# Hybrid RG-LRU / HGRN2 decoder layer on one core: the mixer's instructions noted down and issued in a list-scheduled order, elementwise work moved between engines

## The chip, the core and the metric

One Trainium2 chip, one of its cores. The metric is the device time of one execution in microseconds (us). A core has TensorE (PE: matmuls; PEld is its weight load), VectorE (DVE), ScalarE (ACT), GpSimd (POOL) and SyncE (SP, which here only issues DMAs). Each of them carries out its own instructions strictly in the order of its queue.

## The reference

One decoder layer over x (1024 tokens x 1024 channels, float32):

```python
h = rms_norm(x, norm_mix)
proj = h @ w_in                                  # 1024 -> 8 groups of 1024
xa, ga, q, f, v, g, m_a, m_b = split(proj)
xa = causal_depthwise_conv(xa)                   # width 4
r, i = sigmoid(xa @ w_r + b_r), sigmoid(xa @ w_i + b_i)      # four blocks of 256
log_a = -8 * r * softplus(-lam)
h_t = exp(log_a) * h_(t-1) + sqrt(-expm1(2 * log_a)) * (i * xa)   # RG-LRU
y_a = h * gelu(ga)
f_gate = lb + (1 - lb) * sigmoid(f); k = (1 - lb) * sigmoid(-f)
o = rms_norm(linear attention of silu(q), k, decay f_gate, v)      # HGRN2, 8 heads of 128
y_b = o * silu(g)
x = x + (sigmoid(m_a) * y_a + sigmoid(m_b) * y_b) @ w_out
x = x + square(relu(rms_norm(x) @ w_up)) @ w_down
out = rms_norm(x)
```

## The kernel before

Every float32 matmul is done as three (`mm3`): both operands are split into a high part (ACT, L87) and a rest (DVE, L88). Large products go by a seven-product scheme over 2x2 blocks (`PLAN`): a **quad** is 256 output columns of a weight matrix, cut into four blocks, and takes 7 steps of 12 matmuls of 128x512, 84 in all.

The program has these stages: norm of x and the projection of v; the **mixer**, 28 quads of w_in (`MIX`: XA gives xa for two heads, QF gives q and f of one head, GM gives g and m_b, GA gives m_a and ga); the output projection (`out_proj`, matmuls `po<-wH,y`) with the second norm; MLP up; MLP down with the final norm. `quad_steps` loads the weights of a mixer quad: two tiles are sums of two blocks, made by a load from SP's queue and an accumulating DMA from POOL's queue (`s<-quads_in`, L240 and L241), the rest of the sums is on DVE (L252, L253), then come the splits.

Beside the quads run twelve **tasks** and eight **merges**. `gated_recurrence(p)` (four times) takes two heads of xa: convolution (L441 and L450), gate matmuls (`pr`, `pi`), then sigmoid, exp, tanh, sqrt on ACT with arithmetic between on DVE (L484 to L488), and the scan over time (L498), once for each half of the sequence. `hgrn(u)` (eight times) takes one head of q and f: it folds decays into q and k on DVE (all under `mul`, L506), makes score blocks with small matmuls (`sc`), transposes k (`pk`), makes states (`pkv`, then `ks` on DVE), reads them (`po<-v,scT` and `po<-ks,qf`), norms (squares L692, mean L696, power -1/2 on POOL L697, scaling L699) and transposes back (`poT`), first for the first half of the sequence and then for the second. A task's results go to DRAM (`od`, `hd`), the gates as well (`mad`, `mbd`); `merge(u)` loads them back, multiplies and adds on DVE (L717, L720), splits (L721, L722) and stores `yd`, which `load_y` fetches for the output projection. The tasks use one tile pool `m` with one buffer for each tile name, so a task can begin with a tile only when the task before has let go of it.

The order before is that of the framework's scheduler: it takes the calls in source order, with quad work at a raised priority (`K_EV`, `K_PREP`), and by its own estimate of times.

Of the kernel before, what the change touches and what calls it, by code (L numbers as in the profile page):

```python
# [18 lines left out]
P = 128  # L19
# [35 lines left out]

@with_exitstack
def trunk(ctx: ExitStack, tc: tile.TileContext, x, wts, quads, pv, gains, mask_f, mask_u, out):
    nc = tc.nc
    V, A, G, PE = nc.vector, nc.scalar, nc.gpsimd, nc.tensor

    const = ctx.enter_context(tc.tile_pool(name="const", bufs=1))
    wp = ctx.enter_context(tc.tile_pool(name="wp", bufs=1))
    ps = ctx.enter_context(tc.tile_pool(name="ps", bufs=1, space=PSUM))
    dram = ctx.enter_context(tc.tile_pool(name="dram", bufs=1, space=DRAM))

    def opened(name, **how):
        cm = tc.tile_pool(name=name, bufs=1, reuse_waits="tile", **how)
        return cm.__enter__(), lambda: cm.__exit__(None, None, None)
# [21 lines left out]
    def raw_tile(name):  # L90
        return wp.tile([P, 1024], F32, tag="raw", name=name, bufs=3)

    def load_w(i):
        raw = raw_tile(f"raw{i}")
        nc.sync.dma_start(raw, wts[i])
        return raw
# [124 lines left out]
    def quad_steps(i, pools, raws=raw_tile, singles=2, adding=False):  # L221
# [8 lines left out]
        def load(k):  # L230
            if adding and k == 0:
                raw[k] = pools[0].tile([P, 512], F32, tag="a11", name=f"q{i}{k}")
                nc.sync.dma_start(raw[k], quads[i, k][:, 0:512])
            else:
                raw[k] = raws(f"q{i}{k}")
                nc.sync.dma_start(raw[k], quads[i, k])

        def added(k):
            s[k] = raws(f"s{i}{k}")
            nc.sync.dma_start(s[k][:, 0:512], halves(quads[i, 0])[1])  # L240
            G.dma_start(s[k][:, 0:512], halves(quads[i, 1 - k])[1 - k], accum_op=ALU.add)  # L241
# [46 lines left out]
    hopp, close_hop = opened("hop", side="right")  # L288
    hop = {o: [hopp.tile([P, 4, T], F32R, tag=o + q, name=f"h{o}{q}") for q in ("H", "L")] for _, _, o in PLAN}
# [12 lines left out]
    def load_x(r):  # L302
        x_in[r] = st.tile([P, D], F32, tag="x", name=f"x{r}", bufs=2)
        nc.sync.dma_start(x_in[r], x[r * P : (r + 1) * P, :])
# [34 lines left out]
    nc.sync.dma_start(pvt, pv)  # L339
    nc.sync.dma_start(mf, mask_f)  # L340
    mu32 = st.tile([P, 7, 32], F32, tag="mu32", name="mu32")
    nc.sync.dma_start(mu32, mask_u)
# [15 lines left out]
    def project_v(c, hf, beside):  # L358
# [24 lines left out]
        for tt in range(4):  # L383
            vt = st.tile([P, 512], F32, tag="vt", name=f"vt{c}{hf}{tt}", bufs=2)
            A.copy(vt, pp[tt])
            nc.sync.dma_start(v_d[hf][:, :, 4 * c + tt, :], vt.rearrange("p (h d) -> p h d", h=4))
# [28 lines left out]
    ev, close_ev = opened("ev", side="right")  # L415
    hcar = const.tile([P, 8], F32, tag="hcar", name="hcar")
# [5 lines left out]
    def gated_recurrence(p):  # L422

        xp = [mt(t, f"xp{2 * p + s}", (P, 1792)) for s, t in enumerate(("q1", "qa"))]
        for s in range(2):
            G.memset(xp[s][:, 0:3], 0.0)
            nc.sync.dma_start(xp[s][:, 3 : S + 3], xa_d[2 * p + s])
        wi = mt("v", f"wi{p}", (P, 2, T))
        raw = wi.rearrange("p s t -> p (s t)")
        nc.sync.dma_start(raw, wts[V_TILES + p])  # L430
        wh, wl = (mt(t, f"rg{p}{t}", (P, 1024), F32R) for t in ("ks", "scT"))
        split(raw, wh, wl)
        seg = mt("seg", f"xc{p}", (P, 1536))
        xc = seg[:, 0:1024].rearrange("p (s t) -> p s t", s=2)
        xh = mt("f", f"xcH{p}", (P, 2, T), F32R)
        xl = mt("kk", f"xcL{p}", (P, 2, T), F32R)
        for c in range(NC):
            at = c * T
            for s in range(2):
                u = 2 * p + s  # L440
                V.tensor_scalar(  # L441
                    xc[:, s, :],
# [6 lines left out]
                for j in range(3):  # L449
                    V.scalar_tensor_tensor(  # L450
                        xc[:, s, :],
                        xp[s][:, at + j : at + j + T],
                        pvt[:, PV_CW + 8 * j + u : PV_CW + 8 * j + u + 1],
                        xc[:, s, :],
# [3 lines left out]
            split(xc, xh, xl)  # L458

            parts = [  # L460
                (wi[:, 0, :], wi[:, 1, :], seg[:, 1024:1536], xc[:, 0, :]),
                (*(t[:, 1032 : 1032 + T] for t in xp), m.tile([P, T], F32, tag="o", name=f"e{c}{p}"), xc[:, 1, :]),
            ]
            for s in range(2):
                u = 2 * p + s
                w, ig, e, t = parts[s]
                pr, pi = bank("sc", f"pr{c}{u}"), bank("sc", f"pi{c}{u}")
                for o, k0 in ((pr, 0), (pi, 2)):
                    for k in range(2):
                        cols = slice((k0 + k) * 256 + s * P, (k0 + k) * 256 + (s + 1) * P)  # L470
                        mm3(o, wh[:, cols], wl[:, cols], xh[:, k, :], xl[:, k, :], k == 0, k == 1)
                A.activation(w, pr, AF.Sigmoid, bias=pvt[:, PV_BR + u : PV_BR + u + 1])
                A.activation(ig, pi, AF.Sigmoid, bias=pvt[:, PV_BI + u : PV_BI + u + 1])
                V.tensor_tensor(out=ig, in0=ig, in1=t, op=ALU.mult)


            for s in range(2):
                u = 2 * p + s
                w, ig, e, t = parts[s]
                A.activation(e, w, AF.Exp, scale=sp4n[:, u : u + 1])  # L480
                A.activation(w, w, AF.Tanh, scale=sp4[:, u : u + 1])
            for s in range(2):
                w, ig, e, t = parts[s]
                V.tensor_scalar(w, w, 0.0, None, op0=ALU.max)  # L484
                V.tensor_scalar(e, e, 1.0, None, op0=ALU.add)
# [3 lines left out]
            for s in range(2):  # L489
                w, ig, e, t = parts[s]  # L490
                A.activation(w, w, AF.Sqrt)
            for s in range(2):
                u = 2 * p + s
                w, ig, e, t = parts[s]
# [6 lines left out]
                nc.sync.dma_start(h_d[u][:, at : at + T], h)  # L501

    def hgrn(u):
# [3 lines left out]
        qr = mt("qa", f"qr{nm}", (P, 1792))[:, 0:S]  # L507
        nc.sync.dma_start(qr, q_d[u])
        f = mt("f", f"f{nm}", (P, S))
        kk = mt("kk", f"kk{nm}", (P, S))  # L510
        nc.sync.dma_start(f, f_d[u])
        v = mt("v", f"v{nm}", (P, 8, P))
        nc.sync.dma_start(v, v_d[u // 4][:, u % 4])
        scT = mt("scT", f"scT{nm}", (P, 8, P))
        G.memset(scT, 0.0)
# [5 lines left out]
        V.tensor_scalar(f, f, omlb[:, u : u + 1], lb[:, u : u + 1], op0=ALU.mult, op1=ALU.add)  # L521
        V.tensor_scalar(kk, kk, omlb[:, u : u + 1], None, op0=ALU.mult)
# [83 lines left out]
        qv = qb[:, :, 0:32]  # L606
        for b in range(4):
# [52 lines left out]
        state = lambda n: ks[:, 4 + n % 4, :]  # L660
# [3 lines left out]
        for half in range(2):  # L664
            n0, nkv = 4 * half, 4 - half
            pks.append(bank("hg", f"pk{half}{u}"))
            for n in range(nkv):
                PE.transpose(pks[half][:, n * P : (n + 1) * P], kk[:, (n0 + n) * P : (n0 + n + 1) * P], ident)
        for half in range(2):
            n0, nkv = 4 * half, 4 - half  # L670
            on = mt("on", f"on{half}{u}", (P, 4, P))
            A.copy(ks[:, :nkv, :], pks[half][:, : nkv * P].rearrange("p (n k) -> p n k", n=nkv))
            pkv = bank("sc", f"pkv{half}{u}")
            for n in range(nkv):
                PE.matmul(pkv[:, n * P : (n + 1) * P], ks[:, n, :], v[:, n0 + n, :], start=True, stop=True)
            po = bank("hg", f"po{half}{u}")
            for n in range(4):
                a = n0 + n
                o_ps = po[:, n * P : (n + 1) * P]
                PE.matmul(o_ps, scT[:, a, :], v[:, a, :], start=True, stop=a == 0)  # L680
                if a > 0:
                    PE.matmul(o_ps, qf[:, a * P : (a + 1) * P], state(a), start=False, stop=True)  # L682
                if n < nkv:
                    kv = pkv[:, n * P : (n + 1) * P]
                    if a == 0:
                        V.tensor_copy(state(1), kv)
                    else:
                        V.scalar_tensor_tensor(
# [520 lines left out]
```

## Time and profile before

| what | value |
|---|---|
| three runs | 1695.49, 1706.29, 1712.78 us; median 1706.29 |
| the profiled execution | 1699.1 us, its span 1697.3 us |
| busy in the span | PE 1563.2, DVE 1242.3, ACT 839.5, POOL 128.1 us |
| mean granted TensorE clock | 0.973 |

In the profile a row of a group gives line, engine, operation, output and inputs, shape, count, then busy time in us and mean ns of one, then the idle time of that engine just before them and who ended it. A row of a timeline gives start, duration and the instruction. A stretch `a:b` is in us from the start of the span; in the table of stretches the busy times of the engines follow in the order PE, PEld, DVE, ACT, POOL, then the granted clock, the DMA share and GB/s.

### The profile page before, as it was taken

Reading aid. Unit: us, or ns where it says so; the run is one execution under the profiler, and the core shown is the slowest. Engines: PE = TensorE matmul, PEld = TensorE weight load, DVE = VectorE, ACT = ScalarE, POOL = GpSimd, SP = SyncE. Lnnn points to the kernel's source line nnn. Section 1 sums busy time; section 2 is a strip of 40 time slices with the busy share of each in tenths; the row PEclk is TensorE's granted clock in tenths of the full one; section 3 lists DMA queues with packets and bytes.
Section 4 is the critical chain, followed back from the end, with each engine's and each line's share of the span. In section 5 each row is a group of like instructions: output and inputs, shape, how many; then the busy total and the mean of one; then the engine's idle time right before and its main releaser. Section 6 shows DMA issues by size and latency. Waiting matters only on the chain.

```text
span 1697.3 us, 22898 instructions
## 1 busy us (share of the span) xinstructions
PE 1563.2 (92%) x8520; PEld 1242.5 (73%) x8520; DVE 1242.3 (73%) x1908; ACT 839.5 (49%) x1335; POOL 128.1 (8%) x169
## 2 busy tenths in 40 slices
PE   6999899988899799998999687999999999999998
PEld 4787677766677577776777566788778778888886
DVE  4755687778777786898455259788777798787877
ACT  5644545754476455744433146666766652212213
POOL 0000122111211111112100001000000000000000
PEclk9999999999999999999999798999999999999999
DMA  5554463465444646455357684366566666566652
GB/s 184 163 151 152 130 183 111 121 181 170 147 136 154 175 142 193 125 158 162 116 167 273 224 300 163 124 257 251 226 239 253 237 233 262 223 239 261 248 231 100
DMA packets 110799, 320.96 MB, mean 189 GB/s; under 512 B 11872, under 2 KB 20192, under 8 KB 99936
## 3 DMA queue, kind: packets, MB, share of 16 engines
q1 hardware_dynamic: 101040, 299.05, 49.1%
q0 software_dynamic: 8064, 14.68, 5.4%
q10 hardware_dynamic: 1584, 5.77, 0.9%
q8 instruction: 67, 1.10, 0.3%
q14 instruction: 44, 0.36, 0.1%
HBM read 217.75 MB, written 101.71 MB: 188 GB/s over the span
## 4 chain that ended last, share of the span: by engine, by line
PE 43%; DMA 11%; DVE 9%; ACT 4%; issue 3%; POOL 1%; SPq 0%; DVEq 0%; POOLq 0%; ACTq 0%
PE dX L126 3%; PE dX L128 3%; PE dX L127 3%; PE uX L126 3%; PE uX L127 3%; PE uX L128 3%; DMA q<-quads_in 3%; DMA s<-quads_in 2%; PE dY L128 2%; PE dY L126 2%; PE dY L127 2%; PE uY L128 2%; PE uY L126 2%; PE uY L127 2%; DMA raw<-wts_in 1%
## 5 line engine op out<-in xcount | busy, mean ns | idle before, releaser
L1124 DVE TENSOR_TENSOR acc<-acc,dX 128x512 f32<-128x512 f32 x128 | 85.2, 684 | 31.1 <-PE dX L128 30.4
L87 ACT CAST wA<-q 128x512 fp32r<-128x512 f32 x60 | 37.1, 621 | 137.0 <-PE dX L128 102.4
L241 POOL DMA_DIRECT2D s<-quads_in x56 | 51.5, 920 | 441.0 <-DMA s<-quads_in 124.9
L252 DVE TENSOR_TENSOR s<-s,q 128x512 f32<-128x512 f32 x60 | 41.4, 689 | 56.4 <-DMA s<-quads_in 51.7
L87 ACT CAST wH<-raw 128x1024 fp32r<-128x1024 f32 x40 | 42.0, 1051 | 66.1 <-PE po L127 30.1
L88 DVE TENSOR_TENSOR wL<-raw,wH 128x1024 fp32r<-128x1024 f32 x40 | 48.9, 1223 | 34.8 <-ACT wH L87 34.4
L126 PE MATMUL po<-wH,y 128*128 128x512 f32 x128 | 53.2, 421 | 18.7 <-DMA y<-yd 8.6
L253 DVE TENSOR_TENSOR s<-s,q 128x512 f32<-128x512 f32 x60 | 41.3, 688 | 29.7 <-DMA q<-quads_in 29.5
L88 DVE TENSOR_TENSOR wA<-q,wA 128x512 fp32r<-128x512 f32 x60 | 41.2, 686 | 20.5 <-ACT wA L87 20.5
L1124 DVE TENSOR_TENSOR acc<-acc,dY 128x512 f32<-128x512 f32 x64 | 43.5, 686 | 16.3 <-PE dY L128 15.3
L127 PE MATMUL po<-wL,y 128*128 128x512 f32 x128 | 53.3, 416 | 0.3 <-DVE wL L88 0.3
L128 PE MATMUL po<-wH,y 128*128 128x512 f32 x128 | 52.2, 408 | 0.0
L983 ACT ACTIVATE b<-b 128x512 f32<-128x512 f32 x48 | 30.3, 632 | 36.1 <-DVE b L982 36.1
L126 PEld LDWEIGHTS po<-wH,y 128*128 128x128 f32 x128 | 25.5, 200 | 26.0 <-DMA y<-yd 9.0
L450 DVE SCALAR_TENSOR_TENSOR xc<-xp,pvt,xc 128x512 f32<-128x512 f32 x48 | 35.4, 745 | 0.5
L692 ACT ACTIVATE on<-po 128x128 f32<-128x128 f32 x64 | 16.9, 280 | 28.8 <-PE po L682 28.7
L984 ACT ACTIVATE b<-b 128x512 f32<-128x512 f32 x48 | 30.2, 631 | 1.3
L127 PEld LDWEIGHTS po<-wL,y 128*128 128x128 f32 x128 | 26.0, 203 | 6.5 <-DVE wL L88 1.3
L702 PE MATMUL poT<-ident,on 128*128 128x128 f32 x64 | 18.4, 313 | 13.2 <-ACT on L699 13.2
L128 PEld LDWEIGHTS po<-wH,y 128*128 128x128 f32 x128 | 25.9, 202 | 5.5
L506 DVE TENSOR_TENSOR kk<-kk,seg 128x768 f32<-128x768 f32 (+1 forms) x32 | 26.9, 840 | 3.2 <-PE sc L639 3.2
L717 DVE TENSOR_TENSOR mga<-mga,mgh 128x512 f32<-128x512 f32 x16 | 11.0, 687 | 24.6 <-DMA mga<-mad 24.6
(3086 smaller groups left out, 5365.8 us busy)
## 6 DMA issues: line engine op xcount, KB each, us to landing
q<-quads_in SPq DMA_DIRECT2D x92, 512.0 KB, 4.4
raw<-wts_in SPq DMA_DIRECT2D x40, 512.0 KB, 4.6
s<-quads_in SPq DMA_DIRECT2D x56, 256.0 KB, 2.8
s<-quads_in POOLq DMA_DIRECT2D x56, 256.0 KB, 4.4
y<-yd SPq DMA_DIRECT2D x16, 512.0 KB, 6.0
q<-quads_in SPq DMA_DIRECT2D x28, 256.0 KB, 4.5
x<-x_in SPq DMA_DIRECT2D x8, 512.0 KB, 3.4
vd<-vt SPq DMA_DIRECT2D x16, 256.0 KB, 3.3
```

What stands on the lines that cost most here:

```text
L87: keep(A.copy(h, src))
L88: keep(V.tensor_tensor(out=lo, in0=src, in1=h.bitcast(F32), op=ALU.subtract))
L126: PE.matmul(o, ah, bh, start=first, stop=False, **how)
L127: PE.matmul(o, ah, bl, start=False, stop=False, **how)
L128: PE.matmul(o, al, bh, start=False, stop=last, **how)
L241: G.dma_start(s[k][:, 0:512], halves(quads[i, 1 - k])[1 - k], accum_op=ALU.add)
L252: V.tensor_tensor(out=s2, in0=s1, in1=a11, op=ALU.add)
L253: V.tensor_tensor(out=s4, in0=s2, in1=a12, op=ALU.add)
L450: V.scalar_tensor_tensor(xc[:, s, :], xp[s][:, at + j : at + j + T], pvt[:, PV_CW + 8 * j + u : PV_CW + 8 * j + u + 1], xc[:, s, :], op0=A ...
L983: A.activation(b[:, at, :], b[:, at, :], AF.Relu, scale=-1.0 if at == 2 else 1.0)
L984: A.activation(b[:, at, :], b[:, at, :], AF.Square)
L1124: V.tensor_tensor(out=dst, in0=dst, in1=banks[bk, pr], op=op)
```

## The change

All engine calls of the mixer stage are no longer issued as they are made. A class `Later` stands between and notes each call with its cost in a table of formulas (`cost`), the calls that it depends on, the ring of its tiles, and a date (`due`: quad n by 24 us x (n+1), task k by 40 + 56k, merges by 600). `ordered` then plays the stage through: whenever an engine is free it takes, of the calls that are ready, the one with the earliest date, dates being carried back from call to call. The calls are issued in the order of these starts, and the framework leaves that order as it is. All of them now stand at line L247 in a profile.

Beside that, work changes engine. On POOL in place of DVE: the three elementwise calls of a merge (L717 twice, L720), the first of the four steps of the convolution (L441), and the three `tensor_scalar` calls of a recurrence (L484, L485, L488). On ACT in place of DVE: the two affine steps of `hgrn` (L521, L522). The states and the reads of `hgrn` are regrouped: all keys, then all seven states, then the reads of both halves, then both norms, where before the second half followed the first. In `gated_recurrence` the second half of the sequence has tiles of its own, so that its convolution can come before the recurrence of the first half. The tile ring `raw` and the split activations (`hop`) get other places in memory.

The core of the diff:

```diff
+class Later:
...
+    SETS = {AF.Sigmoid: 1, AF.Exp: 2, AF.Sqrt: 3}
+    TABLE = 1.28
...
+    def cost(engine, method, out, k, aps):
...
+        if method == "dma_start":
+            size = 4 * n * out.ap[0][1]
+            slow = "accum_op" in k
+            return (0.92 if engine == "POOL" else 0.06), 1.9 + size / (1.0e5 if slow else 1.9e5), size / 2.0e5
+        if engine == "PE":
+            t = 0.000456 * n if n >= 256 else 0.11 if n == 128 else 0.0009 * n if n == 64 else 0.02
+            return t, 0.3, 0
+        if engine == "ACT":
+            return 0.15 + 0.00088 * n + 0.08 * (scalars > 0) + 0.21 * ("accum_out" in k), 0.12, 0
+        if engine == "POOL":
+            return (0.2 + 0.00075 * n if method == "memset" else 0.65 + 0.0009 * n), 0.12, 0
+        t = {"tensor_scalar": 0.11 + 0.00063 * n, "tensor_tensor_scan": 0.15 + 0.0022 * n}.get(method, 0.16 + 0.00104 * n)
+        return t + (0.06 if scalars else 0), 0.12, 0
...
+    def ordered(self):
...
+        due = [o[8] for o in ops] + [1e9] * (total - n)
+        for i in reversed(order):
+            due[i] = min([due[i], *(due[j] - seen_by(i, j) for j in succ[i])])
...
+        while done < total:
+            best = None
+            for e in names:
+                at = free[e] if now[e] else max(free[e], soon[e][0][0]) if soon[e] else None
+                if at is not None and (best is None or at < best[0]):
+                    best = (at, e)
+            at, e = best
+            while soon[e] and soon[e][0][0] <= at:
+                _, i = heapq.heappop(soon[e])
+                heapq.heappush(now[e], (due[i], i))
+            _, i = heapq.heappop(now[e])
...
+        return sorted(out, key=lambda i: starts[i])
+
+    def issue(self):
+        self.on = False
+        order = self.ordered()
+        with self.tc.manual_schedule():
+            for i in order:
+                _, _, go, a, k, *_ = self.ops[i]
+                go(*a, **k)
...
 def gated_recurrence(p):
...
-                V.tensor_scalar(
-                    xc[:, s, :],
+                G.tensor_scalar(
+                    xc[c][:, s, :],
...
-                V.tensor_scalar(w, w, 0.0, None, op0=ALU.max)
-                V.tensor_scalar(e, e, 1.0, None, op0=ALU.add)
+                G.tensor_scalar(e, e, 1.0, 1.0, op0=ALU.add, op1=ALU.mult)
+                G.tensor_scalar(w, w, 0.0, 1.0, op0=ALU.max, op1=ALU.mult)
...
-                V.tensor_scalar(e, t, -0.5, -1.0, op0=ALU.mult, op1=ALU.add)
+                G.tensor_scalar(e, t, -0.5, -1.0, op0=ALU.mult, op1=ALU.add)
...
 def hgrn(u):
...
-        V.tensor_scalar(f, f, omlb[:, u : u + 1], lb[:, u : u + 1], op0=ALU.mult, op1=ALU.add)
-        V.tensor_scalar(kk, kk, omlb[:, u : u + 1], None, op0=ALU.mult)
+        A.activation(f, f, AF.Identity, scale=omlb[:, u : u + 1], bias=lb[:, u : u + 1])
+        A.activation(kk, kk, AF.Identity, scale=omlb[:, u : u + 1])
...
+        for half in range(2):
+            values(half)
+        po = [reads(half) for half in range(2)]
+        on = [normed(half, po[half]) for half in range(2)]
+        out(0, on[0])
+        out(1, on[1])
 def merge(u):
...
-                    V.tensor_tensor(out=tf, in0=tf, in1=t["h" if k == "a" else "o"], op=ALU.mult)
+                    G.tensor_tensor(out=tf, in0=tf, in1=t["h" if k == "a" else "o"], op=ALU.mult)
...
-            V.tensor_tensor(out=af, in0=af, in1=bf, op=ALU.add)
+            G.tensor_tensor(out=af, in0=af, in1=bf, op=ALU.add)
...
+    QUAD_PACE, TASK_PACE, TASK_FROM, MERGED = 24.0, 56.0, 40.0, 600.0
...
     for n, (kind, u) in enumerate(MIX):
+        later.due = (n + 1) * QUAD_PACE
...
+        if kind in ("XA", "QF"):
+            tasks += 1
+            later.due = TASK_FROM + tasks * TASK_PACE
+            (gated_recurrence if kind == "XA" else hgrn)(u)
         elif kind == "GA":
+            later.due = MERGED
             merge(u)
-    for close in (close_m, close_w1m, close_ev, close_hop, close_mk):
+    later.issue()

```

Three places show how the order moves. The first is ACT at the end of the first head's `hgrn`: `on<-po` with `hssq` are the squares of the first half, `on<-po,hrs` its scaling by the power that POOL makes in between; the rest are gate and weight pieces of quads. Before:

```order
L692 ACTIVATE on_1697,hssq_1686<-po_1704 128x128 x4
L699 ACTIVATE on_1697<-po_1704,hrs_1687 128x128 x4
L759 ACTIVATE b_5_2975<-b_5_2975 128x512
L704 ACTIVATE ot_1731<-poT_1726,pvt 128x512
L692 ACTIVATE on_1734,hssq_1686<-po_1740 128x128 x4
L594 COPY qb_1960<-qa_1956 128x32x4x2
L699 ACTIVATE on_1734<-po_1740,hrs_1687 128x128 x4
```

and now:

```order
L247 COPY pGAZ_1337<-pGAX_1336 128x512
L247 ACTIVATE on_1165,hssq_1156<-po_1163 128x128 x4
L247 ACTIVATE qf_1153,hssq_1156<-po_1164 128x128 x3
L247 ACTIVATE on_1165<-po_1163,hrs_1157 128x128 x4
L247 ACTIVATE qf_1153,hssq_1156<-po_1164 128x128
L247 COPY e_6_1343<-pGAX_1336 128x512
L247 ACTIVATE ot_1167<-poT_1166,pvt 128x512
L247 ACTIVATE qf_1153<-po_1164,hrs_1157 128x128 x4
```

Between the squares of the first half and their scaling stood nothing before; now the squares of the second half stand there (`qf`, into which the second half is written now), and the scaling of that half waits until a quad's copy and the first half's output are through. On PE, 9 quad matmuls stood between the last read of the first half and the first transpose `poT`; now 22 do. On the whole of ACT, 48 table loads stood in the order; now there are 53.

The second place is POOL in the recurrence of the last pair of heads. `s<-quads_in` are accumulating DMAs for later quads, `hrs` the powers of a norm, `hcar` the carry between the halves, `mga`/`mgb` merge tiles. Before:

```order
L426 MEMSET xp_5767 128x3
L241 DMA s_5764<-quads_in 128x512
L697 TENSOR_TENSOR hrs_5247<-hssq_5246,mhalf 128x4 x2
L241 DMA s_5998<-quads_in 128x512
L241 DMA s_6050<-quads_in 128x512
L500 COPY hcar<-wi_5773 128x1
L500 COPY hcar<-xp_5767 128x1
L241 DMA s_6412<-quads_in 128x512
L241 DMA s_6469<-quads_in 128x512
```

and now:

```order
L247 TENSOR_TENSOR mga_1845<-mga_1845,mgh_1844 128x512
L247 DMA s_1919<-quads_in 128x512
L247 TENSOR_TENSOR hrs_1645<-hssq_1644,mhalf 128x4
L247 TENSOR_SCALAR xc_1728<-xc_1728 128x512
L247 TENSOR_SCALAR wi_1731<-wi_1731 128x512
L247 TENSOR_TENSOR mgb_1847<-mgb_1847,mgo_1846 128x512
L247 TENSOR_TENSOR mga_1845<-mga_1845,mgb_1847 128x512
L247 TENSOR_SCALAR xd_1738<-xp_1726,pvt 128x512
L247 TENSOR_SCALAR xd_1738<-xp_1727,pvt 128x512
L247 TENSOR_SCALAR xc_1728<-xc_1728 128x512
L247 TENSOR_SCALAR e_1741<-e_1741 128x512
L247 COPY hcar<-wi_1731 128x1
```

The queue that held DMAs and a few small instructions now has merges and the steps of the recurrence among them, each with 512 elements in a partition. They stand ahead of the accumulating DMA that follows.

The third place is SP at the end of the mixer. `y<-yd` are the loads for the output projection, `od<-ot` the stores of the last head, `mad<-a` those of the last gate, `mgo`, `mga`, `mgb`, `mgh` loads of the last merge, `raw` the weights of the output projection. Before:

```order
L869 DMA y_7985<-yd_178 128x1024
L723 DMA yd_185<-mgb_7660 128x512
L724 DMA yd_185<-mga_7655 128x512
L869 DMA y_7986<-yd_180 128x1024
L869 DMA y_7987<-yd_182 128x1024
L869 DMA y_7988<-yd_184 128x1024
L95 DMA raw_8014<-wts_in 128x1024
L792 DMA mad_161<-a_27_7889 128x512
L95 DMA raw_8044<-wts_in 128x1024
L799 DMA mad_161<-a_27_7906 128x512
L95 DMA raw_8074<-wts_in 128x1024
```

and now:

```order
L247 DMA mad_167<-a_27_2022 128x512
L247 DMA od_159<-ot_1897 128x512
L247 DMA mgb_2027<-mbd_175 128x512
L1116 DMA y_7996<-yd_186 128x1024
L247 DMA mgo_2026<-od_159 128x512
L247 DMA od_159<-ot_1899 128x512
L1116 DMA y_7997<-yd_188 128x1024
L247 DMA mga_2029<-mad_167 128x512
L1116 DMA y_7998<-yd_190 128x1024
L247 DMA yd_192<-mgb_2027 128x512
L247 DMA yd_192<-mga_2025 128x512
```

Before, seven of the eight loads `y` for the first half of the tokens were issued ahead of the last gate's stores, and the last head had been stored long since. Now the stores of the last head stand among those loads, and three of the loads come behind them. On PE the score matmuls of the last head (`sc`) now begin after 27.3 of the 28 quads, where they had begun after 22.4; its reads stand behind the last quad matmul and right ahead of the output projection.

More of the change, by code (lines that the diff above doesn't have):

```diff
@@ L1 @@
+import heapq
 from contextlib import ExitStack
@@ L426, in gated_recurrence, with convolved @@
             G.memset(xp[s][:, 0:3], 0.0)
[L427 to L432, printed above, removed]
+            SP.dma_start(xp[s][:, 3 : S + 3], xa_d[2 * p + s])
         seg = mt("seg", f"xc{p}", (P, 1536))
[L434 to L437, printed above, removed]
+        xc = [seg[:, 0:1024].rearrange("p (s t) -> p s t", s=2)]
+        def convolved(c):
             at = c * T
@@ L457, in gated_recurrence @@
                     )
[L458 to L464, printed above, removed]
-                u = 2 * p + s
[L466 to L474, printed above, removed]
@@ L699, in hgrn, with out @@
                 A.activation(on[:, n, :], po[:, n * P : (n + 1) * P], AF.Identity, scale=r[:, n : n + 1])
+            return on
+        def out(half, on):
             pt = bank("hg", f"poT{half}{u}")
```

400 lines of the change are left out of this document (287 added, 113 removed).

## The prediction

> **What bounds the kernel now.** I read the table of stages first, because the change touches one of them, the mixer, from its first matmul at 120 to the first matmul of the output projection at 920.
>
> ```profile
> span 1697.3 us, 22898 instructions
> PE 1563.2 (92%) x8520; PEld 1242.5 (73%) x8520; DVE 1242.3 (73%) x1908; ACT 839.5 (49%) x1335; POOL 128.1 (8%) x169
> ...
> 120.00:920.00 800.00, 726.60 (x4939) 572.86 (x4938) 581.42 (x990) 427.19 (x739) 114.36 (x141) 0.97 0.52 156
> 920.00:1053.00 133.00, 105.69 (x441) 84.56 (x439) 73.22 (x95) 50.89 (x74) 4.87 (x7) 0.89 0.71 247
> 1053.00:1376.00 323.00, 316.20 (x1343) 251.67 (x1342) 257.87 (x323) 220.67 (x312) 0.55 (x1) 0.99 0.58 220
> ```
>
> In the mixer PE is busy 726.6 of 800 us and DVE 581.4. So 73.4 us pass with PE idle, and of the busy time 3% (726.6 x 0.03 = 22 us) is lost because the granted clock is 0.97. With no loss at all the mixer would take 800 - 73 - 22 = 705 us. That PE can be kept this busy for long is seen in the stage after 1053, where it is busy 316.2 of 323 us at clock 0.99. All that a better order can win is therefore 95 us. That a matmul itself is not the trouble is seen in its spacing, in a stretch without waits:
>
> ```profile
> 142.32 0.39 PE L126 MATMUL pQFY<-ht1H,ws11H 128*128 128x512 f32 x1
> ...
> 145.12 0.39 PE L126 MATMUL pQFX<-hn2H,ws11H 128*128 128x512 f32 x1
> ```
>
> Twelve matmuls in 2.80 us are 0.233 us each; the 28 x 84 = 2352 of the quads take 549 us, and neither their number nor their shape changes. The small matmuls of the tasks keep their number too.
>
> Then I read whom PE waited for in the mixer:
>
> ```profile
> PE poT L702 <- ACT on L699: 13.2, 11, 2.4
> PE sc L536 <- DVE q L506: 13.1, 4, 6.1
> PE pr L126 <- ACT xcH L87: 11.3, 5, 4.9
> PE sc L536 <- DVE qb L506: 6.9, 4, 3.8
> PE sc L621 <- DVE qb L506: 6.7, 4, 2.2
> PE pGAX L126 <- DVE a L781: 5.6, 4, 2.6
> ```
>
> These are 57 of the 73 us, and 51 of them are waits for a task: the quads stand ready in the queue behind a small matmul whose operand isn't there. No row names weights of a quad. So the loss is one of order, and it sits between PE and the chains on DVE, ACT and POOL.
>
> **The order (the largest term).** The first row is the norm of a head. Its chain from the last read to the first `poT`:
>
> ```profile
> L699 ACT ACTIVATE on<-po,hrs 128x128 f32<-128x128 f32 x64 | 18.6, 371 | 17.7 <-POOL hrs L697 17.7
> L697 POOL TENSOR_TENSOR hrs<-hssq,mhalf 128x4 f32<-128x4 f32 x16 | 18.6, 1162 | 89.1 <-DVE hssq L696 89.1
> L692 ACT ACTIVATE on<-po 128x128 f32<-128x128 f32 x64 | 16.9, 280 | 28.8 <-PE po L682 28.7
> L692 ACT ACTIVATION_READ_ACCUMULATOR on<-po 128x1 f32 x64 | 13.4, 210 | 0.0
> L696 DVE TENSOR_SCALAR hssq<-hssq 128x4 f32<-128x4 f32 x16 | 2.7, 171 | 9.3 <-ACT on L692 9.1
> ```
>
> Four squares with their sums (4 x 0.49 = 2.0, less some overlap), 0.17, 1.16 and four scalings (4 x 0.37 = 1.5) are 4.8 us. Before, 9 quad matmuls (2.1 us) stand on PE in that gap, and the row of waits says up to 2.4 us; now 22 stand there, 5.1 us. So this wait mostly goes: I take 11 of its 13 us. Of the 27 us that `sc` waits for DVE (13.1, 6.9, 6.7) I take half, 14, since DVE's order now follows dates, but DVE stays as loaded as it was (below). Of the 11.3 us of `pr` I take 8: the first gate matmul stands after 3.0 quads instead of 1.7. Of the rest of the 73 us I take 8. That is 41 us of 73 won. The bounds are nothing and all 73.
>
> What the order gives back: after 26.0 quads, score blocks, transposes, states and reads of the seventh head stand on PE with no quad matmul between. That is three hand-overs to DVE or ACT in a row, and the row of `sc` L621 gives 2.2 us as the longest of one; I take 6 us. The clock: the lost 22 us come in stretches of lower clock beside idle PE, so with about half of the idle time left I take half, 11. Five more table loads on ACT at 1.283 us are 6.4 us on an engine that is busy 427 of 800; that cover makes them free, and if they all fell on the path they would cost those 6.
>
> **The moved work.** These rows leave DVE:
>
> ```profile
> L717 DVE TENSOR_TENSOR mgb<-mgb,mgo 128x512 f32<-128x512 f32 x14 | 9.6, 688 | 9.9 <-DMA mgb<-mbd 7.7 <-issue 2.1
> L441 DVE TENSOR_SCALAR xc<-xp,pvt 128x512 f32<-128x512 f32 x16 | 8.7, 543 | 3.7 <-DMA xp<-xad 3.7
> L485 DVE TENSOR_SCALAR xc<-xc 128x512 f32<-128x512 f32 x8 | 3.4, 425 | 8.3 <-ACT xc L480 8.3
> L521 DVE TENSOR_SCALAR f<-f,par 128x1024 f32<-128x1024 f32 x8 | 6.4, 801 | 0.0
> L522 DVE TENSOR_SCALAR kk<-kk,par 128x1024 f32<-128x1024 f32 x8 | 6.0, 750 | 2.9 <-ACT kk L518 2.9
> ...
> L519 ACT ACTIVATE f<-f 128x1024 f32<-128x1024 f32 x8 | 8.5, 1062 | 0.0
> ```
>
> 48 calls of the merges at 0.688 (33.0 us), 16 of the convolution at 0.543 (8.7), 48 of the recurrence at 0.425 (20.4) and 16 affine steps (12.4): 74 us of DVE's 581. ACT gets 16 x 1.06 = 17 us, which lie beside a PE that has its quads, and 17 is what they cost if they all came to lie on a chain that PE waits for. The second half's own tiles, the later load of `v` and the new places in memory I cost at nothing: no row of PE's waits names them, and a late tile would show there as a wait of a task's first matmul. POOL gets 112 calls of 512 elements. The trace has no such call; its nearest rows, and what DVE did meanwhile, are
>
> ```profile
> 632.00 0.24 POOL L586 TENSOR_SCALAR seg<-seg 128x32 f32<-128x32 f32 x1 [1.60 <-DVE seg L506]
> 783.31 0.41 POOL L586 TENSOR_SCALAR seg<-seg 128x128 f32<-128x128 f32 x1
> 461.06 1.78 POOL L608 TENSOR_SCALAR scT<-dd 32x256 f32<-32x256 f32 x4 [1.02 <-DVE dd L580]
> 295.68 3.30 POOL L608 TENSOR_SCALAR scT<-dd 32x256 f32<-32x256 f32 x4 [4.86 <-DVE dd L580]
> ...
> 295.43 0.68 DVE L506 TENSOR_TENSOR qb<-qb,seg 128x512 f32<-128x512 f32 x1
> 297.83 0.88 DVE L506 TENSOR_TENSOR qb<-qb,seg 128x512 f32<-128x512 f32 x1
> ```
>
> From 32 to 128 elements a call grows by 0.17 us for 96, so for 512 I get 0.24 + 480 x 0.0018 = 1.1 us; the 256 elements of `scT` at 1.78/4 = 0.45 would give 0.9, four times the 128 would give 1.6. I take 1.1, near the first: 123 us more on POOL, 237 of some 740. That is cover enough for POOL itself.
>
> The last four rows show the price. Alone, four copies take 1.78 us; beside DVE's products of two operands 3.30, and the product itself 0.88 in place of 0.68. So the two engines hold each other up: DVE loses 0.20 us for a POOL call of 0.45, 45% of it. At 45% of 1.1 us, for some 70% of 112 calls (DVE is busy 581 of 800), DVE loses 0.45 x 1.1 x 112 x 0.7 = 39 us of its 74. The bounds are 0 and 112 x 1.1 = 123 us, which would be 49 more than was taken off. The net of 35 us is not on the path by itself, since PE and not DVE sets the end; it is part of why I take half of the `sc` waits, and a POOL call that takes twice as long delays the recurrence, which has three in a row with DVE, but no quad waits for that.
>
> The Trainium skill has a rule against this part: "SBUF — State Buffer", section "Who interferes with whom", says that a VectorE instruction with two SBUF inputs contends with a GpSimd instruction that reads SBUF and that the later one blocks until the other is done. The rows above agree in kind (3.30 against 1.78 us); taken in full for every call the sum would have DVE's 123 us in place of 39, the upper bound already given. The consequence is weighed as the second rival.
>
> **The end of the mixer.** The last head's reads now come right behind the last quad matmul, and PE waits for its states: I take 4 us. Then the output projection begins, and before it already waited there for the last merge:
>
> ```profile
> PE po L126 <- DMA y<-yd: 8.6, 1, 8.6
> ...
> od<-ot SPq DMA_DIRECT2D x16, 256.0 KB, 2.3
> mgo<-od SPq DMA_DIRECT2D x16, 256.0 KB, 3.8
> yd<-mga SPq DMA_DIRECT2D x16, 256.0 KB, 2.4
> y<-yd SPq DMA_DIRECT2D x16, 512.0 KB, 6.0
> ```
>
> The chain from the last reads: norm 4.8, transpose, copy and second half some 5, store 2.3, load 3.8, two POOL calls and an add 3, split 1.3, store 2.4, load 6.0: about 29 us, against 84 matmuls or 19.6 us that need no last merge. Three loads `y` stand behind the last head's stores on SP, but those are out 18 us before the chain ends. So the wait of 8.6 becomes about 10. I take 5 us more for the whole end; the bounds are 0 and the whole chain of 29 uncovered.
>
> **The sum,** against the profiled execution of 1699.1 us (1697.3 and 1.8 around it): 41 + 11 won, less 6, less 5: 41 us, 1658. One thing more pushes down. DVE is unevenly loaded before:
>
> ```profile
> DVE  4755687778777786898455259788777798787877
> ```
>
> In the slices from the fifth to the nineteenth, which are the mixer with tasks (a slice is 42 us), the digits are 6 to 9, mostly 7 and 8, in the twentieth and the two behind it 4 and 5: the last 100 us of the mixer had no tasks, and now they have. Where DVE has more room PE waits for it less, and I put this at 13 us, a third of the 43 that remain of 95 after 41 + 11; the bounds are nothing and those 43. That gives 1645. The median of the runs, 1706.29, is 7 us above the profiled execution, and the runs spread over 17, so 1% is what can be told from no change; I keep 1645, which is 3.6% below the median.
>
> **The rivals.** *First, PE is filled.* The order rests on durations close to the trace's (0.15 + 0.00088 x 1024 = 1.05 us for an ACT call of 1024 elements, where the row has 1.062; 0.000456 x 512 = 0.233 for a matmul). Then the loss of 95 us falls to 10 to 20, and the end costs nothing: 1699 - 85 to 1699 - 75, about 1619. Against it: one late operand stops a strictly ordered queue, and the list doesn't know of the 3.30 against 1.78. Chance 0.2. *Second, slower: POOL and DVE block each other on the path.* If DVE loses 1.1 us for every call, it has 581 - 74 + 123 = 630 us of work. At the share that it reached before, 581 of 800, that takes 867 us, at the share of the best stretches (8 tenths) 788. With calls stretched to 2 us in the recurrence and the accumulating DMAs queued behind them, quads would wait for weights as well. It decides from 0.66 us of blocking per call (74/112), where DVE has more to do than before; at 1.1 I get between 788 and 867, about 827, so 1725. This is what the rule of the Trainium skill would come to here if each call blocked for its whole length; the rows with a price, 0.88 against 0.68, say 0.45 of it. Chance 0.1. *Third, the waits only move:* the order is planned with times that the chip doesn't keep, and the single buffers of the tasks and the late last heads keep the length. Then 1690 to 1710; PE idle stays near 73 us. Chance 0.13. My forecast has the remaining 0.57, with its own range from 1626 to 1688.
>
> **Range and chances.** Low 1605 takes in most of the first rival; high 1708 takes in the third. Faster by over 1% means below 1689: forecast, first rival and a little of the third, 0.78. Within 1%: 0.13. Slower: 0.09.
>
> **What would show it.** The first quad matmul of the mixer to the first `po<-wH,y` should fall from 800 to 740 to 755 us; PE's waits there from 73 to about 40, those of `poT` for `on` below 3 us; granted clock 0.98 to 0.99; DVE busy near 545; POOL's 512-element calls at 1.1 us alone and about 2 beside DVE. The stages after 1053 keep their lengths of 323 and 322 us. I'm wrong if PE waits for weights `ws` of quads, if POOL passes 350 us of busy time, or if the output projection grows by more than 15 us.

## The result, and the profile after

The median went from 1707.74 us (1695.49 to 1712.78, four runs) to 1636.17 us (1634.88 to 1640.74, four runs): a ratio of 0.960, 95% interval 0.954 to 0.965. The forecast was 1645 us, in a range from 1605 to 1708. The profiled execution took 1640.74 us; the forecast was worked out from the profiled one before, 1699.1 us, so its sum of 54 us stands against 58.4.

First the busy times from the page after, then the stages (mixer, output projection, the rest) and the mixer cut where the matmuls of 21 quads are done, from the table of stages:

```profile
span 1639.0 us, 22939 instructions
PE 1551.2 (95%) x8520; PEld 1238.0 (76%) x8520; DVE 1232.0 (75%) x1780; ACT 859.8 (52%) x1356; POOL 273.2 (17%) x281
```

```profile
119.50:864.15 744.65, 716.72 (x4930) 568.78 (x4928) 578.24 (x870) 445.44 (x748) 250.31 (x246) 0.98 0.57 167
864.15:990.56 126.41, 102.87 (x448) 83.49 (x449) 65.86 (x85) 52.51 (x84) 13.94 (x14) 0.89 0.78 264
990.56:1639.00 648.44, 630.26 (x2699) 505.81 (x2697) 517.82 (x705) 297.64 (x424) 0.55 (x1) 0.99 0.58 222
...
119.50:633.80 514.30, 505.68 (x3298) 402.63 (x3297) 387.58 (x572) 302.13 (x487) 163.58 (x162) 0.99 0.58 169
633.80:864.15 230.35, 211.04 (x1634) 166.15 (x1632) 190.66 (x298) 143.30 (x261) 86.72 (x84) 0.94 0.53 162
```

The mixer of the kernel before, cut at the same matmul:

```profile
120.00:732.39 612.39, 555.27 (x3752) 437.85 (x3751) 458.29 (x779) 347.07 (x582) 90.85 (x113) 0.97 0.51 151
732.39:920.00 187.61, 171.33 (x1189) 135.00 (x1188) 123.12 (x212) 80.12 (x158) 23.51 (x28) 0.96 0.56 171
```

The mixer fell from 800 to 744.7 us and the output projection from 133 to 126.4. PE idle in the mixer fell from 73.4 to 27.9 us, and all of that was won in the first 21 quads: there it fell from 57.1 to 8.6 us, though DVE is busy for the same 75% of the time in both. The last seven quads and the tail have 19.3 us of idle time, where they had 16.3, and the low clock: four of the eight heads are normed there, where two were, and DVE is 83% busy there, where it was 66%.

PE's waits in the mixer, the longest of the list:

```profile
PE pXAX L247 <- DVE r L247: 3.2, 2, 2.3
PE pXAY L247 <- ACT e L247: 2.6, 1, 2.6
PE pGMX L247 <- ACT wA L247: 2.4, 1, 2.4
...
PE sc L247 <- DVE q L247: 2.1, 1, 2.1
...
PE po L327 <- DMA y<-yd: 1.8, 1, 1.8
```

The waits of `poT` for `on` (13.2 us) and of `pr` for `xcH` (11.3) have left the list, and those of `sc` for DVE are down to 2.4 us a row or less. Nothing in the mixer is waited for longer than 2.6 us at once. What is left is of another kind: before, 61 of the 73 us were waits of a task's small matmuls; now quad matmuls wait for 17 of the 28, and 7.5 of these are for weights (`wA`, `wA1225L`, `ws124H`). The wait for `y` goes on behind the mixer: 1.8 us at its end and 2.9 later, 4.7 together.

What did not come is the relief of VectorE. Two stretches of its timeline and the same of POOL's:

```profile
297.73 1.78 DVE L247 TENSOR_TENSOR kk<-kk,f 128x512 f32<-128x512 f32 x1
...
302.13 1.88 DVE L247 TENSOR_TENSOR qb<-qb,seg 128x512 f32<-128x512 f32 x1
```

```profile
297.25 1.72 POOL L247 TENSOR_TENSOR mga<-mga,mgh 128x512 f32<-128x512 f32 x1 [2.44 <-DMA mga<-mad]
...
301.90 1.56 POOL L247 TENSOR_TENSOR mgb<-mgb,mgo 128x512 f32<-128x512 f32 x1
```

A product `qb<-qb,seg` of 128x512, 0.68 us before, takes 1.88 beside a merge on POOL. Over the whole execution DVE should have fallen by the 74 us that left it, from 1242.3 to 1168; it stands at 1232.0. So 64 us came back as stretching, calls that take longer than they did: 64/112 = 0.57 us for each call on POOL, if all of it is POOL's doing (the first experiment leaves 57).

### The profile page after: what moved, and what is told of

Same layout as the page of the kernel before. It is cut to its first block, busy times and chain, and to the rows that moved or that the text cites. A ratio compares the mean times of both kernels' runs of the same rounds, so it can differ in the third digit from the quotient of the medians.

```text
span 1639.0 us, 22939 instructions
## 1 busy us (share of the span) xinstructions
PE 1551.2 (95%) x8520; PEld 1238.0 (76%) x8520; DVE 1232.0 (75%) x1780; ACT 859.8 (52%) x1356; POOL 273.2 (17%) x281
## 4 chain that ended last, share of the span: by engine, by line
PE 74%; DVE 9%; DMA 7%; ACT 6%; issue 3%; POOL 1%; SPq 0%; DVEq 0%; POOLq 0%; ACTq 0%
PE pQFX L247 5%; PE pGMX L247 5%; PE pGAX L247 4%; PE dX L327 4%; PE dX L329 4%; PE dX L328 4%; PE uX L327 3%; PE uX L328 3%; PE uX L329 3%; PE pGMY L247 3%; DMA raw<-wts_in 2%; PE pQFY L247 2%; PE sc L247 2%; PE pGAY L247 2%; PE dY L329 2%
## 5 line engine op out<-in xcount | busy, mean ns | idle before, releaser
L288 ACT CAST wA<-q 128x512 fp32r<-128x512 f32 x33 | 20.4, 621 | 139.4 <-PE dX L329 102.7
L247 POOL DMA_DIRECT2D s<-quads_in x52 | 46.6, 901 | 158.7 <-DMA s<-quads_in 46.0
L247 DVE TENSOR_TENSOR s<-s,q 128x512 f32<-128x512 f32 x54 | 43.5, 806 | 11.6 <-DMA s<-quads_in 8.1
L247 DVE TENSOR_TENSOR qb<-qb,seg 128x512 f32<-128x512 f32 (+1 forms) x40 | 27.3, 683 | 17.0 <-PE sc L247 16.2
L247 DVE TENSOR_TENSOR kk<-kk,seg 128x768 f32<-128x768 f32 (+1 forms) x32 | 29.3, 915 | 9.3 <-PE sc L247 9.3
L247 PEld LDWEIGHTS sc<-qb,kk 128*32 128x32 f32 (+1 forms) x896 | 21.3, 116 | 19.7 <-issue 16.6
L289 DVE TENSOR_TENSOR wA<-q,wA 128x512 fp32r<-128x512 f32 x33 | 22.6, 686 | 14.9 <-ACT wA L288 14.9
L247 PE MATMUL sc<-qb,kk 128*32 128x48 f32 (+2 forms) x896 | 27.3, 211 | 4.8 <-DVE dd L247 2.4
L247 POOL TENSOR_SCALAR scT<-dd 32x256 f32<-32x256 f32 x32 | 19.9, 621 | 60.8 <-DVE dd L247 48.0
L1150 PE MATMUL xT_h<-ident,xn_h 128*128 128x128 f32 x64 | 10.7, 323 | 20.0 <-DVE xn_h L351 13.0
```

The source lines that it names most:

```text
L247: go(*a, **k)
L288: keep(A.copy(h, src))
L289: keep(V.tensor_tensor(out=lo, in0=src, in1=h.bitcast(F32), op=ALU.subtract))
L1150: PE.transpose(pt[:, k * P : (k + 1) * P], xn[:, (4 * h + k) * P : (4 * h + k + 1) * P], ident)
```

## The experiments

**Theory A** was: the order carries the gain, and what POOL takes over is paid back by the two engines holding each other up. **The rival:** VectorE's relief carries a good part of it. Ratios are to the kernel before, run on the same chip. The experiments are from three sets of runs (first to fourth, fifth to eighth, ninth to twelfth), each on a chip of its own; between sets, and against the changed kernel, the ratios are the better measure than the medians.

*First: everything that went to POOL back on VectorE.*

```diff
-                G.tensor_scalar(e, e, 1.0, 1.0, op0=ALU.add, op1=ALU.mult)
+                V.tensor_scalar(e, e, 1.0, 1.0, op0=ALU.add, op1=ALU.mult)
...
-            G.tensor_tensor(out=af, in0=af, in1=bf, op=ALU.add)
+            V.tensor_tensor(out=af, in0=af, in1=bf, op=ALU.add)
```

> All 112 calls that the change gave to POOL stand on VectorE again (the first step of the convolution, three calls of each recurrence, three of each merge); the list schedule, the two affine steps on ACT and all tiles stay. Theory A (the order carries the gain, and what POOL took off VectorE was paid back by the two holding each other up, 71 of 74 us): DVE busy in the mixer gets 62 us of calls back and loses about 112 x 0.63 = 71 us of stretching, so near 570 us, where the changed kernel had 578; the time is that of the changed kernel, 1628 to 1646 us. Theory B (the relief of VectorE carries a good part of the gain): DVE busy near 640 us, the last quads starve, 1660 to 1690 us.

1634.38 us, ratio 0.960 (0.955 to 0.964): the changed kernel's time with none of its calls on POOL. Theory A holds. From this kernel's page, and its mixer in the table of stages:

```profile
PE 1545.5 (95%) x8520; PEld 1233.8 (76%) x8520; DVE 1237.2 (76%) x1892; ACT 859.2 (53%) x1358; POOL 136.3 (8%) x169
...
120.02:857.50 737.48, 704.83 (x4915) 560.94 (x4914) 576.75 (x969) 441.74 (x735) 119.22 (x139) 0.99 0.55 167
```

PE idles 32.7 us in the mixer, so the list without POOL's help wins 40.7 of the 73.4. The 16 affine steps stay on ACT here, so DVE should have 1242.3 - 12.4 = 1229.9 us; it has 7.3 more with nothing moved to POOL. So 57 of the 64 us go with the calls on POOL, 0.51 each.

*Second: only the merges back on VectorE* (the two `G.tensor_tensor` lines of `merge`).

> Only the 48 calls of the merges stand on VectorE again, the 64 others stay on POOL. Theory A: 33 us of calls come back and about 48 x 0.63 = 30 us of stretching go; DVE busy 575 to 585 us, time 1630 to 1645 us. Theory B: DVE busy near 610 us, 1648 to 1670 us. A third case: if products of two operands are what blocks VectorE, and calls with one operand hardly do, DVE busy falls below 565 us and the time below 1630 us.

1614.64 us, 0.950 (0.946 to 0.953): the third case, 20 us faster than the first experiment.

```profile
PE 1537.0 (95%) x8520; PEld 1231.6 (76%) x8520; DVE 1223.6 (76%) x1828; ACT 855.5 (53%) x1355; POOL 210.9 (13%) x233
```

The pages price the calls. From all back (1237.2) to this one 64 one-operand calls, 29.1 us of work, leave DVE, and it falls by 13.6: 15.5/64 = 0.24 us of stretching each. From here to the changed kernel 48 two-operand calls, 33.0 us, leave, and DVE rises by 8.4: 41.4/48 = 0.86 us each, more than the 0.69 that the call costs on VectorE itself. One kind pays, the other doesn't, and the sum was nothing. DVE's busy time differs by up to 4.6 us between kernels with the same division of work (the second, the seventh and the eleventh), so these prices are good to about 0.1 us.

*Third: the moved work in the framework's order* (`later.on` stays False, nothing is issued from the list, and the two blocks of `high_priority(1000)` stand again).

> The same instructions, engines and tiles as the changed kernel, but handed to the framework's own order, with the priority of 1000 for a quad's evictions and preparation as before; nothing is noted down. Theory A (order): PE idle in the mixer goes back to near 70 us, the waits of poT for on and of pr for xcH are there again, and the time is 1690 to 1715 us; POOL and DVE hold each other up here too, so it is no faster than the kernel before. Theory B (the moved work and the shorter chains carry the gain): 1640 to 1665 us.

1727.49 us, 1.016 (1.012 to 1.020): slower than before, so theory A holds for the order, and the time is above what either theory gave. The mixer in its table of stages:

```profile
119.70:952.27 832.57, 716.74 (x4938) 566.93 (x4936) 549.90 (x872) 437.41 (x753) 251.90 (x247) 0.97 0.50 150
```

PE idles 115.8 us. DVE is less busy than in the kernels so far (1202.9 over all) and yet waited for more: busy time was not what counted. Here the stretching is 1202.9 - 1168 = 35 us. The longest of PE's waits in this mixer that bear on the two theories:

```profile
PE pGAX L327 <- DVE e L995: 8.4, 3, 3.9
PE pGAX L327 <- ACT e L1064: 7.8, 2, 5.3
PE pQFX L327 <- DVE r L981: 6.6, 2, 5.2
PE pr L327 <- ACT xcH L288: 6.5, 4, 4.3
PE pr L328 <- DVE xcL L289: 5.3, 3, 2.6
PE poT L938 <- ACT on L932: 5.0, 7, 1.2
...
PE poT L938 <- ACT qf L932: 4.3, 6, 1.0
```

The waits of `pr` and `poT` are there again, as theory A had it. What has grown most is of the kind of the first three rows: quad matmuls wait 39.5 us in all for DVE and ACT, which first have to take earlier products of quads out of their tiles (into `e`, `r`), against 11.8 us in the kernel before.

*Fourth: the calls on POOL shortened in the same order.*

```diff
+                if engine == "POOL" and method in ("tensor_scalar", "tensor_tensor") and tuple(out.shape) == (P, T):
+                    if not any(tuple(v.shape) == (P, 1) for v in a if hasattr(v, "tensor")):
+                        cut = lambda v: v[:, 0:1] if hasattr(v, "tensor") else v
+                        a, k = [cut(v) for v in a], {n: cut(v) for n, v in k.items()}
```

> The same order on every engine, but 96 of the 112 calls on POOL (recurrences and merges, not the convolution) work on one column of 512, so that they cost about 0.2 us each; the other 511 columns are left out of these steps. Theory A (POOL's calls stretch VectorE's by about 0.63 us each): DVE busy in the mixer falls by about 60 us, from 578 to near 518, POOL's by 90 to 110; the last seven quads, which lose 41 us, lose about half, and the time is 1608 to 1628 us. Theory C (VectorE's calls are longer for another reason, such as the denser traffic of DMA and ACT in the new order): DVE busy stays at 565 to 578 us and the time within 8 us of the changed kernel.

1613.95 us, 0.949 (0.946 to 0.953). DVE falls by 45.7 us, 0.48 for each shortened call (60 were expected), with its own instructions untouched: this much of the stretching is POOL's doing.

*Fifth: the merges on POOL with one operand.* The rival to the operand was the place: a VectorE that is full in the last quads.

```diff
+                if engine == "POOL" and method == "tensor_tensor" and tuple(k["out"].shape) == (P, T):
+                    go, a, k = self.tc.nc.gpsimd.tensor_scalar, (k["out"], k["in0"], 0.5, 0.0), dict(op0=ALU.mult, op1=ALU.add)
```

> As the changed kernel, in the same order; only the 48 products and sums of the merges, which stay on POOL, take one operand (a multiplication by a constant, in place; the second operand is left out). Theory A2 (what blocks VectorE is a POOL call with two operands: putting these 48 back on VectorE gave it 33 us of work and made it 15.6 us less busy, so each costs it 1.0 us, against about 0.25 us of the others): DVE busy in the mixer falls by about 36 us, to 535 to 550, and the time to 1610 to 1624 us. Rival D (it is the place, beside a VectorE that is full in the last quads, and any call of this length would do it): DVE busy 568 to 580 us, time 1628 to 1644 us.

1621.40 us, 0.953 (0.950 to 0.957). DVE is at 1206.5, 25.5 below the changed kernel (36 were expected): (1206.5 - 1223.6 + 33.0)/48 = 0.33 us of stretching a call where two operands cost 0.86. The calls themselves, the answer for this tile on POOL (shortest, median and longest in ns) in the changed kernel and in this one:

```profile
L247 POOL TENSOR_TENSOR mga<-mga,mgh x16: 1262/1472/2030, 297.2 to 887.0; 128x512 f32<-128x512 f32 x16
```

```profile
L249 POOL TENSOR_SCALAR mga<-mga x32: 607/933/1771, 295.5 to 872.8; 128x512 f32<-128x512 f32 x32
```

A call with two operands is twice as long (1.26 against 0.61) and stretches VectorE some 2.6 times as much. The time of this run can't be put down to that alone, since the merges here don't wait for the load of the second operand either.

*Sixth: the maxima back on VectorE too* (one more line, `G.tensor_scalar(w, w, 0.0, ...)`).

> The merges on VectorE as in the second experiment, and also the 16 calls of the recurrences that take a maximum; 48 one-operand calls are left on POOL. On POOL a maximum over 512 takes 1.92 us even undisturbed, where a multiplication with an addition takes 0.62. Theory A3 (POOL's length is hidden, only VectorE's own time counts): DVE gets 16 x 0.43 = 7 us and loses 4 of stretching, time within 5 us of the 1614.6 of the second experiment, 1610 to 1620 us. Rival E (the slow maximum holds up the recurrences, and with them every later task): 1598 to 1608 us.

1626.17 us, 0.955 (0.953 to 0.958): 12 us slower than with the maxima on POOL (10 by the ratios), outside both expectations, though DVE grew by 2.4 us only. The list had laid out another order, with `pr` waiting 4.8 us for `xcH`.

The maxima also answer whether it is the length of a POOL call that stretches VectorE, and not its second operand. A maximum has one operand and takes 1.92 us. At the merges' price by length (0.86 us for 1.26) each would cost 1.3 us, and DVE would be 14 us less busy with all 16 taken back. It is 2.4 us busier here, and 1.4 and 0.1 us busier in the other two pairs with equal dates (the twelfth against the seventh, the eighth against the eleventh). With 6.8 us of calls come back, that is 0.28 to 0.42 us of stretching for a call: near the other calls with one operand.

*Seventh: other dates, with the merges on VectorE.* The dates here and below were found by trying many in the list's own plan.

```diff
-            later.due = TASK_FROM + tasks * TASK_PACE
+            later.due = TASK_DUE[tasks - 1]
```

> The merges on VectorE as in the second experiment, and other dates: the last three tasks are due at 581, 631 and 687 in place of 600, 656 and 712, the sixth at 382 in place of 376, and the merges at 660 in place of 600. Theory F (what is lost in the last seven quads, 25 us in the second experiment, is a pile of tasks that the dates let come late): these quads lose 8 to 15 us less, 1600 to 1608 us. Rival G (the tasks are held by their single buffers and by VectorE's load, not by dates): 1611 to 1619 us.

1607.61 us, 0.945 (0.942 to 0.947), 7 us less: theory F at the edge of its range. The last seven quads and the tail idle 8.5 us, where they idled 17.7 in the second experiment.

*Eighth: the maxima on VectorE too, with dates for that.*

> The maxima and the merges on VectorE, and dates found for this division: tasks due at 80, 140, 202, 258, 320, 376, 426, 483, 544, 577, 651, 713, merges at 660, 23.75 for each quad. If theory F holds and the maxima cost nothing: 1598 to 1608 us; if E holds as well: 1590 to 1600 us; if neither: 1610 to 1620 us.

1600.56 us, 0.941 (0.938 to 0.943): the fastest, 2% below the changed kernel. The mixer takes 701.5 us, 14.2 of them idle:

```profile
119.45:820.99 701.54, 687.31 (x4878) 553.23 (x4877) 562.12 (x910) 431.79 (x725) 155.08 (x187) 0.99 0.59 174
```

That left open whether the dates or the maxima did it, and whether POOL is needed at all. The four last runs ask this.

*Ninth: nothing on POOL, with dates for that.*

> All 112 calls on VectorE as in the first experiment, with dates found for that division (tasks due at 96, 146, 214, 264, 300, 356, 381, 461, 474, 511, 665, 675; merges at 600; 23.75 for each quad). Theory H (with good dates the one-operand calls on POOL still relieve VectorE, by the 20 us between the first and the second experiment): 1612 to 1630 us. Rival I (with good dates nothing needs to leave VectorE): 1596 to 1608 us.

1604.91 us, 0.944 (0.941 to 0.946): rival I. With dates of its own the kernel with nothing moved to POOL is 4.4 us slower than the fastest, their intervals overlapping. The whole mixer, and its part behind 21 quads, in its table of stages:

```profile
121.11:825.11 704.00, 686.67 (x4879) 552.04 (x4877) 570.89 (x958) 433.15 (x727) 108.63 (x139) 1.00 0.58 174
...
652.86:825.11 172.25, 167.57 (x1177) 133.35 (x1175) 151.15 (x249) 110.56 (x173) 25.35 (x30) 1.00 0.64 200
```

The late stretch idles 4.7 us at full clock, where the changed kernel's idles 19.3 at 0.94 and the first experiment's, with the same division, 16.4 at 0.97.

*Tenth: the changed kernel with two other dates.*

> The changed kernel with all its moved work, two dates changed: the tenth task due at 576 in place of 600, the merges at 660 in place of 600. Theory A2 (a two-operand call on POOL costs VectorE 1.0 us wherever it stands): only the dates win, 7 to 13 us as between the second and the seventh experiment, 1622 to 1630 us, DVE busy in the mixer 570 to 580. Rival J (it was the place: merged later, the calls fall where VectorE has room): 1600 to 1614 us, DVE below 560.

1619.83 us, 0.953 (0.950 to 0.955): two dates win 16 us by the medians, just below A2's range, and 12 by the ratios, whose intervals just touch. The last seven quads and the tail idle 12.2 us in place of 19.3. DVE stays at 572.2 in the mixer, as A2 has it (1231.1 over all, 1232.0 in the changed kernel): the stretching doesn't go with the place.

*Eleventh and twelfth: the dates of the seventh and the eighth exchanged.*

> The division of the seventh experiment (merges on VectorE, maxima on POOL) with the dates of the eighth. If the maxima on POOL are what the eighth is faster by: 1605 to 1611 us. If dates serve only the division for which they were found: 1612 to 1624 us.

> The division of the eighth experiment (merges and maxima on VectorE) with the dates of the seventh. If the maxima on POOL cost time by themselves, the eighth's time or a little more: 1598 to 1606 us. If dates serve only the division for which they were found: 1614 to 1630 us.

1616.00 us (0.950, 0.948 to 0.953) and 1626.39 us (0.956, 0.954 to 0.958). With exchanged dates both divisions are back where the plain dates had them (1614.64 and 1626.17). So in these two pairs dates serve only the division for which they were found; the maxima alone explain nothing.

## Why the prediction was right, and where it was off

- **The order** was the right term. Idle time fell by 45.5 us, where 41 won, less 6 given back, and 13 from levelling make 48. All of it came from the first 21 quads, 57.1 to 8.6 us. `poT` and `pr` won all of their 13 and 11, a little more than the 11 and 8 taken. That the order did it and not the moved work is shown for `pr`: with the list and nothing on POOL (first experiment) no wait of it is left, with the moved work in the framework's order (third) for 15 us. For `poT` it is shown in part: 5.9 us are left in the mixer of the first, 9.3 in the third.
- **The levelling of VectorE** was wrong in kind. Its 13 us were to come from a VectorE with more room once the end of the mixer had tasks too. In the first 21 quads VectorE kept its share of 75%; the tasks pile up at the end, and 19.3 of the 27.9 us that are left lie there, 3 more than before. Dates alone take that to 12.2 us (tenth experiment), and to 4.7 from 16.4 with nothing on POOL (ninth against first).
- **The clock** came out at 0.98; 716.7 x 0.02 = 14 us are lost instead of 22, so 8 won for 11.
- **The total** is near for a reason that is partly luck: the order won 48.5 us in the first 21 quads, where 35 net were taken, and that and the end of the mixer made up for the levelling.
- **The moved work** was mis-sized: 39 us of stretching forecast, 64 measured, of which 57 go with the calls on POOL; DVE's busy time in the mixer is 578 us for the 545 forecast. The 45% of a POOL call that VectorE was to lose came from one-operand copies; it was taken for products too. In the old order the stretching is 35 us, near the forecast; that more calls meet because the list packs the engines is likely, but not shown. A POOL call was 0.61 us with one operand and 1.26 with two, and 1.92 for a maximum, not 1.1 for all; POOL's busy time in the mixer, 250 us, came near 237 only because these cancel.
- **The second rival** had its mechanism right: 0.51 us of blocking per call against the 0.66 from which it decides, and 0.86 for the merges alone. It did not decide: in the first 21 quads PE idles only 8.6 us, whatever the cause. The rule that the prediction weighed, the Trainium skill's "SBUF — State Buffer", section "Who interferes with whom" (the later of the two blocks until the other is done), gives the upper bound. In the rows shown, 1.88 against 0.68 us beside a POOL call of 1.56, the product loses 77% of that call. The average of a merge, 0.86 us for a call of 1.47, is 59%, between the 45% and the whole.
- **The end of the mixer** had the wrong sign: 5 us more were forecast. The wait for `y` fell from 8.6 to 4.7 us, PE waited 1.2 us for the last states where 4 were taken, and the output projection fell by 6.6.
- **The first rival** (PE is filled) asked too much of these dates: 28 us of idle time and 14 of clock are left, where it had 10 to 20 in all. With dates for its division the ninth experiment has 17.3 us of idle time at clock 1.00.
- **The third rival** (waits only move) fell: no PE wait in the mixer is longer than 2.6 us.
- **Weights** were one of the signs of being wrong, and it shows in small: quads wait 7.5 us for them, 2.4 at most at once, where no wait named them before. The stages behind the output projection take 648.4 us (644.3 before, 4 us more).

What stays open: why results of the quads come late in the framework's order with the moved work, though VectorE is less busy there; how much of the order's gain the two halves of a head have; and what the two affine steps on ACT and the new tiles and places in memory are worth, which every experiment kept.

## What to carry to other kernels

Waits spread over many chains are a matter of order: a list that schedules by dates won 4%, and its dates a further 2%, while the work moved to POOL won nothing that better dates did not also give. Here PE lost its idle time with VectorE as busy as before, so a busy share alone does not tell what an order can win. Price work for POOL by its operands and by what VectorE does meanwhile, and compare divisions only with dates fitted to each, since moving 16 calls of one kind made a difference of 10 to 12 us.

## What was not expected of the hardware

A maximum over 512 elements on POOL is three times as long as a multiplication with an addition, in two rows next to each other in the changed kernel:

```profile
186.39 0.61 POOL L247 TENSOR_SCALAR xc<-xc 128x512 f32<-128x512 f32 x1 [1.36 <-ACT xc L247]
187.14 1.94 POOL L247 TENSOR_SCALAR wi<-wi 128x512 f32<-128x512 f32 x1
```

On VectorE, in the first experiment, the two steps are equal:

```profile
L247 DVE TENSOR_SCALAR xc<-xc 128x512 f32<-128x512 f32 x8 | 3.4, 426 | 4.5 <-ACT xc L247 4.3
L247 DVE TENSOR_SCALAR wi<-wi 128x512 f32<-128x512 f32 x8 | 3.4, 423 | 0.0
```

And a one-operand call on POOL does stretch VectorE's calls, by 0.24 to 0.33 us on average (0.28 to 0.42 for a maximum), against 0.86 for a call with two operands.
